# A two-layer hybrid encoder on one core: Gelu's polynomial on ScalarE, one softmax pass for both key heads, and other warm-up products

## The chip, the cores and the metric

The kernel runs on one core of a Trainium2 chip. The metric is the device time of one execution in microseconds (us), as the median of several runs. A core has TensorE (PE in the rows; its weight loads are PEld), VectorE (DVE), ScalarE (ACT), GpSimd (POOL) and SyncE (SP), which issues the transfers. Each engine works off its own list of instructions in order, and waits on semaphores where an input, or a buffer to write into, isn't ready.

## The reference

Two layers over 512 prompt frames and 8 x 16 sample frames, width 1024, all in float32. Each layer normalizes, projects, sends three parts of the projection through three mixers, projects back, and adds a squared-ReLU MLP:

```
def _hybrid_layer(x, ...):
    proj = _rms_norm(x, norm1) @ w_in                       # 1024 -> 1536
    out_a = _rglru_mixer(u_a, g_a, ...)                     # h * gelu(gate)
    out_b = _s5_mixer(u_b, ...)                             # z = gelu(y); z * sigmoid(z @ w_glu + b)
    out_c = _swa_prompt / _swa_cached(_rope(q), _rope(k), v, sinks)
    x = x + concat([out_a, out_b, out_c]) @ w_out
    x = x + square(relu(_rms_norm(x, norm2) @ w_up)) @ w_down

def _sink_softmax(scores, sinks, mask):
    m = max(max(scores), s);  e = exp(scores - m)
    return e / (sum(e) + exp(s - m))
```

Attention has 8 query heads and 2 key heads (4 query heads on each), chunks of 64 frames, and a window of the chunk itself and the two before it. `gelu` is the tanh form: 0.5 x (1 + tanh(0.798 (x + 0.0447 x^3))).

## The kernel before

**Tiling.** The frames are cut into two groups g of 320 columns (256 of the prompt, 64 of the samples). Activations lie with features on the 128 partitions. A product of one weight tile of 1024 x 128 with a group (`product`, L246) is 24 matmuls of 128x128 by 320 columns: weights and activations are each split into a rounded part and a rest (wh and wl; ScalarE copies wh at L243, VectorE subtracts for wl at L244), and three of the four cross products are added over 8 tiles of the inner dimension. There are 336 such products, 8064 of these matmuls ("mm" in the rows), the same in both kernels.

**Stages.** Layer 0: `in_proj` of group 0 (12 products), its mixers, `in_proj` of group 1 (12 more; 576 matmuls in all), its mixers, `out_proj` of group 0 (8 products), a first quarter of group 0's MLP, `out_proj` of group 1, and the rest of the MLP. Layer 1 does the same, with its first projection and group 0's mixers laid over the end of layer 0's MLP. The mixers are `lru` (L641), `s5` (L694) and `attention` (L788). An output-projection product reads the mixers' result `mix` in eight tiles: tiles 0 to 3 hold the two recurrent mixers, 4 to 7 attention's heads. A product can so begin its first 12 matmuls before attention is done, and three products can do this at once, since the PSUM tag "mm" has three banks.

**Attention** works in chunks cq = 0 to 3 of a group, and on two pairs of samples (hf). `probs(cq, kv)` makes the scores of one key head (L878), and `soft` (L814) the softmax over them: maxima (L818), the negated maximum with the sink (L820 or L822), two exponentials with their sums (L824), the sink's exponential (L826, or L828 and L829), the sum and its reciprocal (L830, L831), and two multiplications, one on VectorE and one on GpSimd (L833). `turned(cq, kv)` transposes the probabilities on TensorE (L176) and copies them back (L890 or L892); `values(cq)` multiplies them by the values (L899) and writes `mix` (L903, L904). The PSUM tag "att", with two banks, serves scores, transposes, values and the gates of `lru` (L663).

**Gelu** (`gelu2`, L542) is called 16 times, on 128x320: two gates and two S5 outputs for each group of each layer. It takes three VectorE operations (L545 to L547), a ScalarE tanh (L548) and a last VectorE operation (L549).

**Setup.** Layer 0's constants for S5 are made on VectorE, GpSimd and TensorE in the first 130 us, beside the projections. Twelve products of a zeroed 128x128 tile (L990) run on TensorE before the first weights arrive.

**Order.** The program is built by a scheduler that plans each engine's list from the code's order and from its own estimates of times. A change in one place so reorders the lists around it.

## Time and profile before

| | |
|---|---|
| median of 3 runs | 1457.65 us (1455.84 to 1466.05) |
| span of the profiled execution | 1454.2 us |
| TensorE busy | 1404.7 us (97%) |
| TensorE weight loads | 1336.3 us (92%) |
| VectorE busy | 924.5 us (64%) |
| ScalarE busy | 662.4 us (46%) |
| GpSimd busy | 377.0 us (26%) |
| mean granted TensorE clock | 0.979 |

The span reaches from the first to the last instruction; a run's time holds a few us more. "Busy" counts the time in which at least one instruction of the engine is under way. TensorE's matmuls overlap, so a busy share of 97% doesn't mean that it does 97% of what it could; how many matmuls a stretch holds tells that. The granted clock is 1.00 at 2.4 GHz and 0.50 at 1.2 GHz.

### The profile page before, as it was taken

The numbers are of one execution on the slowest core, as the hardware profiler recorded it, in microseconds if no ns is written. First come the engines' busy times: TensorE is split into PE (matmuls) and PEld (weight loads), VectorE is DVE, ScalarE is ACT, GpSimd is POOL, SyncE is SP. The second block draws the span as 40 slices with busy tenths as digits, with TensorE's granted clock in tenths as the row PEclk, the third lists the DMA queues.
The fourth block names the chain that finished last, engine by engine and source line by source line (L and its number), as shares of the span: only waits on it lengthen the run. The fifth ranks groups of instructions, "written<-read, shape, count | busy, mean of one in ns | idle before, by whom it ended". The sixth has DMA issues, their size and how long they took to land.

```text
span 1454.2 us, 25829 instructions
## 1 busy us (share of the span) xinstructions
PE 1404.7 (97%) x9540; PEld 1336.3 (92%) x9540; DVE 924.5 (64%) x1858; ACT 662.4 (46%) x1387; POOL 377.0 (26%) x565
## 2 busy tenths in 40 slices
PE   7699999999999999999999999999999999999997
PEld 7688688899999999999987898789999999999997
DVE  8999889856544344357687768875664434434564
ACT  6566565545422122135674667453543312313543
POOL 3847269401010011072244225320110100100111
PEclk9999899999999999999998999899999999999998
DMA  6232122344422222234422342224443222223452
GB/s 244 86 109 81 50 95 97 105 150 140 152 80 78 76 80 73 73 107 157 140 91 73 120 137 92 68 95 145 149 146 106 73 73 73 80 78 104 153 174 94
DMA packets 91389, 156.27 MB, mean 107 GB/s; under 512 B 14336, under 2 KB 18304, under 8 KB 91264
## 3 DMA queue, kind: packets, MB, share of 16 engines
q1 hardware_dynamic: 91264, 154.63, 32.0%
q8 instruction: 75, 1.23, 0.4%
q14 instruction: 50, 0.41, 0.1%
HBM read 151.02 MB, written 3.37 MB: 106 GB/s over the span
## 4 chain that ended last, share of the span: by engine, by line
PE 80%; DVE 11%; POOL 4%; issue 3%; ACT 2%; DMA 1%; SPq 0%; DVEq 0%; POOLq 0%
PE mm L254 24%; PE mm L252 24%; PE mm L253 24%; DVE wl L244 2%; PE att L899 1%; PE att L878 1%; PE s L755 1%; PE s L753 1%; PE att L176 1%; PE s L176 1%; PE fin L326 0%; PE att L663 0%; PE s L721 0%; PE s L779 0%; DVE bigr L269 0%
## 5 line engine op out<-in xcount | busy, mean ns | idle before, releaser
L254 PE MATMUL mm<-bigr,wl 128*128 128x320 f32 x2688 | 840.9, 314 | 22.6 <-DVE wl L244 22.6
L252 PE MATMUL mm<-bigr,wh 128*128 128x320 f32 x2688 | 840.2, 313 | 1.7 <-ACT wh L243 1.1
L253 PE MATMUL mm<-bigr,wh 128*128 128x320 f32 x2688 | 839.1, 313 | 1.0 <-DVE bigr L269 1.0
L243 ACT ACTIVATE wh<-raw 128x512 fp32r<-128x512 f32 x544 | 340.7, 630 | 494.4 <-PE mm L253 469.9
L254 PEld LDWEIGHTS mm<-bigr,wl 128*128 128x128 f32 x2688 | 509.8, 190 | 34.7 <-DVE wl L244 27.4
L252 PEld LDWEIGHTS mm<-bigr,wh 128*128 128x128 f32 x2688 | 509.4, 190 | 7.9 <-issue 5.0
L253 PEld LDWEIGHTS mm<-bigr,wh 128*128 128x128 f32 x2688 | 509.5, 190 | 6.9 <-issue 3.9
L244 DVE TENSOR_TENSOR wl<-raw,wh 128x512 fp32r<-128x512 f32 x544 | 399.7, 736 | 179.6 <-ACT wh L243 158.9
L156 POOL TENSOR_SCALAR bigr<-t 128x320 fp32r<-128x320 f32 x128 | 63.0, 493 | 566.3 <-ACT t L952 566.3
L934 DVE TENSOR_TENSOR xT<-xT,mm 128x320 f32<-128x320 f32 x160 | 77.7, 486 | 127.5 <-PE mm L254 127.4
L952 ACT ACTIVATE t<-t 128x320 f32<-128x320 f32 x128 | 59.9, 470 | 137.9 <-DVE t L951 132.3
L954 DVE TENSOR_TENSOR bigr<-t,bigr 128x320 fp32r<-128x320 f32 x128 | 69.7, 546 | 69.6 <-POOL bigr L156 69.3
L951 DVE SCALAR_TENSOR_TENSOR t<-mm,r 128x320 f32<-128x320 f32 x124 | 60.6, 488 | 81.5 <-PE mm L254 81.4
L288 POOL TENSOR_TENSOR ss<-ss,sq 128x320 f32<-128x320 f32 x58 | 56.9, 981 | 195.7 <-ACT sq L281 185.6
L833 POOL TENSOR_SCALAR att<-att,st 128x192 f32<-128x192 f32 (+3 forms) x40 | 37.2, 931 | 79.5 <-DVE st L831 43.6
L824 ACT ACTIVATE att<-att,st 128x192 f32<-128x192 f32 (+3 forms) x80 | 30.7, 389 | 28.3 <-DVE st L822 22.1
L269 DVE SCALAR_TENSOR_TENSOR bigr<-xT,sm,bigr 128x320 fp32r<-128x320 f32 x64 | 39.7, 629 | 3.8 <-ACT bigr L268 3.6
L268 ACT ACTIVATE bigr<-xT,sm 128x320 fp32r<-128x320 f32 x64 | 34.4, 558 | 11.1 <-DVE xT L934 7.8
L281 ACT ACTIVATE sq<-xT 128x320 f32<-128x320 f32 x66 | 30.4, 460 | 9.9 <-DVE xT L934 3.7
L878 PE MATMUL att<-kT,q 64*64 64x192 f32 (+2 forms) x256 | 28.1, 329 | 2.5 <-ACT att L824 2.1
L605 POOL TENSOR_TENSOR sw<-sw,cs 128x320 f32<-128x320 f32 x20 | 19.4, 969 | 33.6 <-ACT sw L604 28.3
L176 PE MATMUL att<-ident,att 128*128 128x128 f32 (+1 forms) x144 | 24.6, 280 | 3.2 <-DVE att L833 1.0
(287 smaller groups left out, 1078.6 us busy)
## 6 DMA issues: line engine op xcount, KB each, us to landing
raw<-w_up SPq DMA_DIRECT2D x192, 256.0 KB, 2.6
raw<-w_down SPq DMA_DIRECT2D x192, 256.0 KB, 2.6
raw<-w_in SPq DMA_DIRECT2D x96, 256.0 KB, 2.6
raw<-w_out SPq DMA_DIRECT2D x64, 256.0 KB, 2.5
xT<-x SPq DMA_DIRECT2D x8, 320.0 KB, 5.7
yT<-xT SPq DMA_DIRECT2D x8, 320.0 KB, 2.5
cs<-rope SPq DMA_DIRECT2D x4, 320.0 KB, 4.4
gg<-gg SPq DMA_DIRECT2D x2, 512.0 KB, 5.1
```

What stands on the lines that cost most here:

```text
L156: return G.tensor_scalar(out, in_, 1.0, 0.0, OP.mult, OP.add)
L176: PE.transpose(out, in_, ident[0:n, 0:n])
L243: act(h, raw, AF.Copy)
L244: tt(l, raw, h.bitcast(F32), OP.subtract)
L252: mm(pt, lhsT=h[:, k % 4], rhs=m[:, k, 0], start=k == 0, stop=False)
L253: mm(pt, lhsT=h[:, k % 4], rhs=m[:, k, 1], start=False, stop=False)
L254: mm(pt, lhsT=l[:, k % 4], rhs=m[:, k, 0], start=False, stop=k == 7)
L288: G.tensor_tensor(self.ss, self.ss, sq, OP.add)
L934: tt(xT[:, g, k], xT[:, g, k], pt, OP.add)
L951: V.scalar_tensor_tensor(t, pt, 0.0, norm.r, OP.max, OP.mult)
L952: act(t, t, AF.Square)
L954: tt(am[:, f, 1], t, am[:, f, 0].bitcast(F32), OP.subtract)
```

## The change

Three edits. `gelu2` takes a ScalarE square with a scale, one VectorE operation, the tanh and the last VectorE operation, so two VectorE operations fewer and one ScalarE operation more in each call. `soft` takes the scores of both key heads (or of both pairs of samples) in a list: it keeps a maximum for each, and does the small operations on four columns at once in place of two. `sprobs` and `probs` therefore make both sets of scores, in both "att" banks, before the softmax, and the calls at the end of `attention` are reordered. The warm-up is now 20 products over a zeroed tile of 640 columns, which GpSimd clears and ScalarE copies first.

```
@@ gelu2
-        eng.tensor_tensor(w, x, x, OP.mult)
-        eng.tensor_scalar(w, w, 0.044715, 1.0, OP.mult, OP.add)
-        eng.tensor_tensor(w, w, x, OP.mult)
+        act(w, x, AF.Square, scale=math.sqrt(0.044715))
+        eng.scalar_tensor_tensor(w, w, 1.0, x, OP.add, OP.mult)
         act(w, w, AF.Tanh, scale=0.7978845608028654)
         V.scalar_tensor_tensor(out, w, 1.0, x, OP.add, OP.mult)
@@ soft(b, x, sk, nsk, one): b and x are now lists
-            st4 = tp.tile([128, 5, 2], F32, tag="st4", name="st4", bufs=4)
+            st4 = tp.tile([128, 5, 4], F32, tag="st4", name="st4", bufs=2)
-            V.reduce_max(mx, b, axis=AX.X)
+            n2 = 2 * len(b)
+            for m in range(len(b)):
+                V.reduce_max(mx[:, 2 * m:2 * m + 2], b[m], axis=AX.X)
...
-            for n in range(2):
-                act(x[:, n], b[:, n], AF.Exp, scale=0.125, bias=nm[:, n:n + 1], accum_out=den[:, n:n + 1])
+            for n in range(n2):
+                act(x[n // 2][:, n % 2], b[n // 2][:, n % 2], AF.Exp, scale=0.125, bias=nm[:, n:n + 1], accum_out=den[:, n:n + 1])
...
-            for n in range(2):
-                (G if n else V).tensor_scalar(x[:, n], x[:, n], rd[:, n:n + 1], None, OP.mult)
+            for n in range(n2):
+                v = x[n // 2][:, n % 2]
+                (G if n % 2 else V).tensor_scalar(v, v, rd[:, n:n + 1], None, OP.mult)
@@ probs(cq): both key heads, scores in both banks; sprobs() likewise for both pairs of samples
+            bs = [bank3("att", 2, 256) for kv in range(2)]
...
+            soft([b[:, :, 0:nk] for b in bs], [pe[:, :, st:256] for pe in pes], skp[:, L], nskp[:, L], False)
@@ end of attention
-        sprobs(0)
-        sprobs(1)
-        sturned(0)
-        probs(0, 0)
-        sturned(1)
-        svalues(0)
-        svalues(1)
-        probs(0, 1)
+        sprobs()
+        for hf in range(2):
+            sturned(hf)
+        for hf in range(2):
+            svalues(hf)
+        probs(0)
         for cq in range(4):
             for kv in range(2):
                 turned(cq, kv)
-                if cq < 3:
-                    probs(cq + 1, kv)
+            if cq < 3:
+                probs(cq + 1)
             values(cq)
@@ warm-up
-    for _ in range(12):
+    zr = bigr()
+    zr = zr[:, 0:1].rearrange("p a b c -> p (a b c)")
+    G.memset(tab[:, 512:1152], 0.0)
+    act(zr, tab[:, 512:1152], AF.Copy)
+    for n in (512, 384, 320, 256, 128):
+        for _ in range(4):
+            mm(warm[:, 0:n], lhsT=zr[:, 0:128], rhs=zr[:, 0:n], start=True, stop=True)
+    for _ in range(0):
         mm(warm[:, 0:128], lhsT=Mm[...], rhs=Mm[...], start=True, stop=True)
```

Two places show how the lists move. The first is TensorE's list in layer 0 while group 0's attention ends. All 576 input-projection matmuls and the first half of one output-projection product stand ahead of it. `att<-ident,att` are transposes of probabilities, `att<-kT,q` scores, `att<-att,vt` values; rows beginning with `s` in the second name are S5's. Before:

```order
L176 MATMUL att<-ident,att 128x128 x4
L176 MATMUL s_1206<-ident,bigf 128x80 x4
L779 MATMUL s_1226<-bigf,gg 128x320
L878 MATMUL att<-kT,q 64x192 x4
L899 MATMUL att<-att,vt 64x256 x4
L779 MATMUL s_1230<-bigf,gg 128x320
L176 MATMUL att<-ident,att 128x128 x4
L779 MATMUL s_1226<-bigf,gg 128x320
L779 MATMUL s_1230<-bigf,gg 128x320
```

The changed kernel, from the scores of the third chunk (cq = 2) to the first of those of the fourth:

```order
L884 MATMUL att<-kT,q 64x192 x8
L176 MATMUL s_1214<-ident,bigf 128x80 x4
L778 MATMUL s_1233<-bigf,gg 128x320
L778 MATMUL s_1237<-bigf,gg 128x320
L905 MATMUL att<-att,vt 64x256 x2
L778 MATMUL s_1233<-bigf,gg 128x320
L778 MATMUL s_1237<-bigf,gg 128x320
L176 MATMUL att<-ident,att 128x128 x5
L176 MATMUL s_2096<-ident,ub 80x128 x4
L176 MATMUL att<-ident,att 128x128 x3
L176 MATMUL s_2102<-ident,ub 80x128 x4
L884 MATMUL att<-kT,q 64x192 x4
```

Before, this piece holds the last scores of the fourth chunk, and that chunk's alone come behind the 576 matmuls; now those of both heads of the third chunk and of the fourth do. Between the third chunk's scores and the transposes that need its softmax stand four S5 transposes, four S5 products and two value products.

The second place is VectorE's list at the S5 outputs of the same group, where Gelu and softmax stand side by side. Before:

```order
L545 TENSOR_TENSOR gw<-bigf 128x320
L546 TENSOR_SCALAR gw<-gw 128x320
L547 TENSOR_TENSOR gw<-gw,bigf 128x320
L818 TENSOR_REDUCE st_1452<-att 128x2
L549 SCALAR_TENSOR_TENSOR bigf<-gw,bigf 128x320
L822 SCALAR_TENSOR_TENSOR st_1452<-st_1452,nskp 128x2
L828 TENSOR_TENSOR st_1452<-sm,st_1452 128x2
L892 COPY att<-att 128x512
L762 SCALAR_TENSOR_TENSOR bigf<-ub,sm,s_1206 128x320
L830 TENSOR_TENSOR st_1452<-st_1452 128x2
```

After:

```order
L819 TENSOR_REDUCE st_1404<-att 128x2 x2
L761 SCALAR_TENSOR_TENSOR bigf<-ub,sm,s_1214 128x320
L823 SCALAR_TENSOR_TENSOR st_1404<-st_1404,nskp 128x4
L829 TENSOR_TENSOR st_1404<-sm,st_1404 128x4
L546 SCALAR_TENSOR_TENSOR gw<-gw,bigf 128x320
L831 TENSOR_TENSOR st_1404<-st_1404 128x4
L832 RECIPROCAL st_1404<-st_1404 128x4
L548 SCALAR_TENSOR_TENSOR bigf<-gw,bigf 128x320
L835 TENSOR_SCALAR att<-att,st_1404 128x192 x2
```

One Gelu stands there with two VectorE rows in place of four, and one softmax with four columns serves both key heads, with two reductions ahead of it and two multiplications behind.

## Rows read from the trace of the kernel before

**Rows 1.** Page, part 2: busy tenths and granted clock in 40 slices of 36.4 us.

```profile
DVE  8999889856544344357687768875664434434564
PEclk9999899999999999999998999899999999999998
```

**Rows 2.** Windows: stretch, us, each engine's busy us (instructions), granted clock, DMA.

```profile
77.00:147.00 70.00, 65.90 (x469) 59.02 (x468) 68.64 (x167) 47.87 (x120) 43.05 (x62) 0.93 0.29 92
151.00:161.00 10.00, 9.67 (x51) 7.38 (x52) 8.10 (x23) 4.88 (x17) 3.00 (x7) 0.50 0.32 105
161.00:181.00 20.00, 19.67 (x132) 13.45 (x131) 15.28 (x40) 10.04 (x27) 2.66 (x4) 1.00 0.04 14
200.00:252.00 52.00, 48.02 (x324) 41.50 (x323) 51.59 (x85) 26.87 (x69) 47.19 (x58) 0.90 0.28 89
472.61:509.00 36.39, 36.39 (x250) 36.39 (x249) 11.81 (x21) 6.33 (x10) 0.00 (x0) 1.00 0.24 76
```

**Rows 3.** TensorE's waits, 0 to 150 us: who waited for whom, total, times, longest.

```profile
PE mm L254 <- DVE wl L244: 14.2, 12, 2.7
```

**Rows 4.** TensorE's waits from 740 to 990 us (layer 1's mixers).

```profile
PE mm L254 <- DVE wl L244: 3.0, 1, 3.0
```

**Rows 5.** Lines, VectorE, 0 to 300 us: count, busy us, mean ns, idle before.

```profile
L818 DVE TENSOR_REDUCE st<-att 128x2 f32<-128x384 f32 x12 | 6.6, 549 | 2.2 <-PE att L878 2.2
L830 DVE TENSOR_TENSOR st<-st 128x2 f32<-128x2 f32 x20 | 5.9, 297 | 0.9 <-ACT st L829 0.9
L822 DVE SCALAR_TENSOR_TENSOR st<-st,nskp 128x2 f32<-128x2 f32 x16 | 4.7, 292 | 0.1
L828 DVE TENSOR_TENSOR st<-sm,st 128x2 f32<-128x2 f32 x16 | 3.8, 239 | 0.2
L546 DVE TENSOR_SCALAR gw<-gw 128x320 f32<-128x320 f32 x8 | 3.3, 410 | 0.1
L831 DVE RECIPROCAL st<-st 128x2 f32<-128x2 f32 x20 | 3.2, 158 | 0.3
L545 DVE TENSOR_TENSOR gw<-t 128x320 f32<-128x320 f32 x4 | 2.4, 596 | 0.1
```

**Rows 6.** Lines, ScalarE, 60 to 300 us.

```profile
L824 ACT ACTIVATE att<-att,st 128x192 f32<-128x192 f32 x24 | 9.8, 413 | 12.0 <-DVE st L822 10.1 <-DVE rsq L309 1.8
L824 ACT ACTIVATION_READ_ACCUMULATOR att<-att,st 128x1 f32 x40 | 7.8, 196 | 0.0
L281 ACT ACTIVATE sq<-xT 128x320 f32<-128x320 f32 x7 | 3.2, 463 | 2.5 <-DVE xT L934 2.1 <-POOL tab L436 0.4
```

**Rows 7.** Timeline: two heads' softmaxes, first and last rows; TensorE behind the second (start, duration).

```profile
103.69 0.28 DVE L818 TENSOR_REDUCE st<-att 128x2 f32<-128x128 f32 x1
112.70 0.84 POOL L833 TENSOR_SCALAR att<-att,st 128x64 f32<-128x64 f32 x1 [0.26 <-DVE st L831]
...
165.62 0.56 DVE L818 TENSOR_REDUCE st<-att 128x2 f32<-128x384 f32 x1 [1.45 <-PE att L878]
170.26 0.76 POOL L833 TENSOR_SCALAR att<-att,st 128x192 f32<-128x192 f32 x1 [8.45 <-PE att L878]
172.67 1.34 PE L779 MATMUL s<-bigf,gg 128*128 128x320 f32 x4
```

**Rows 8.** Timeline, two neighbouring products at the lower clock.

```profile
158.58 0.47 PE L254 MATMUL mm<-bigr,wl 128*128 128x320 f32 x1
158.84 0.47 PE L252 MATMUL mm<-bigr,wh 128*128 128x320 f32 x1
```

**Rows 9.** Timeline of the start: the warm-up, and TensorE's waits behind it.

```profile
1.75 0.53 POOL L216 MEMSET Mm<- 128x512 f32 x1
2.33 5.39 PE L990 MATMUL fin<-Mm 128*128 128x128 f32 x24 [2.33 <-POOL uap L647]
...
18.27 0.42 PE L254 MATMUL mm<-bigr,wl 128*128 128x320 f32 x1 [1.56 <-DVE wl L244]
```

More of the change, by code (lines that the diff above doesn't have):

```diff
@@ L831, in soft, with sprobs @@
             V.reciprocal(rd, rd)
-            for n in range(2):
-                (G if n else V).tensor_scalar(x[:, n], x[:, n], rd[:, n:n + 1], None, OP.mult)
-        def sprobs(hf):
-            b = bank3("att", 2, 256)
-            for i in range(2):
-                for kv in range(2):
-                    mm(b[64 * kv:64 * kv + 64, i, 0:144], lhsT=q.qS[64 * kv:64 * kv + 64, 2 * hf + i].rearrange("p i t -> p (i t)"),
-                       rhs=kcT[64 * kv:64 * kv + 64, hf, i], start=True, stop=True)
-            soft(b[:, :, 0:144], p[hf], sks[:, L:L + 1], nsks[:, L:L + 1], True)
+            for n in range(n2):
+                v = x[n // 2][:, n % 2]
+                (G if n % 2 else V).tensor_scalar(v, v, rd[:, n:n + 1], None, OP.mult)
+        def sprobs():
+            bs = [bank3("att", 2, 256) for hf in range(2)]
+            for hf, b in enumerate(bs):
+                for i in range(2):
+                    for kv in range(2):
+                        mm(b[64 * kv:64 * kv + 64, i, 0:144], lhsT=q.qS[64 * kv:64 * kv + 64, 2 * hf + i].rearrange("p i t -> p (i t)"),
+                           rhs=kcT[64 * kv:64 * kv + 64, hf, i], start=True, stop=True)
+            soft([b[:, :, 0:144] for b in bs], p, sks[:, L:L + 1], nsks[:, L:L + 1], True)
         def sturned(hf):
@@ L867, in geo, with probs @@
             return j, ((1,) if j == 0 else (0, 1)), nk, 64 * max(cc - 2, 0), 256 - nk, 64 - 64 * ch
-        def probs(cq, kv):
+        def probs(cq):
             j, kts, nk, k0, st, w0 = geo(cq)
-            pe, ps, q0 = pes[kv], slice(64 * kv, 64 * kv + 64), 64 * cq
+            q0 = 64 * cq
             if cq == 0:
-                G.memset(pe[:, :, 0:64], 0.0)
-                G.memset(pe[:, :, 256:320], 0.0)
-            b = bank3("att", 2, 256)
+                for pe in pes:
+                    G.memset(pe[:, :, 0:64], 0.0)
+                    G.memset(pe[:, :, 256:320], 0.0)
+            bs = [bank3("att", 2, 256) for kv in range(2)]
             for pr in range(2):
                 for s in range(2):
-                    mm(b[64 * s:64 * s + 64, pr, 0:nk], lhsT=q.q[ps, 2 * pr + s, q0:q0 + 64], rhs=kT[ps, k0:k0 + nk], start=True, stop=True)
-            soft(b[:, :, 0:nk], pe[:, :, st:256], skp[:, L, 2 * kv:2 * kv + 2], nskp[:, L, 2 * kv:2 * kv + 2], False)
+                    for kv, b in enumerate(bs):
+                        ps = slice(64 * kv, 64 * kv + 64)
+                        mm(b[64 * s:64 * s + 64, pr, 0:nk], lhsT=q.q[ps, 2 * pr + s, q0:q0 + 64], rhs=kT[ps, k0:k0 + nk], start=True, stop=True)
+            soft([b[:, :, 0:nk] for b in bs], [pe[:, :, st:256] for pe in pes], skp[:, L], nskp[:, L], False)
         def turned(cq, kv):
```

## The prediction

> **What bounds the kernel now.** I read the page's slices first, then windows by stage, then TensorE's waits, and last the groups of instructions and a timeline. The slices [rows 1] show VectorE at nine tenths or near it for the first 290 us and at 5 to 8 tenths from 650 to 1020 us (both times the mixers run), and mostly at 3 to 5 elsewhere. In the MLP stretches TensorE does nothing but its products: 250 in 36.39 us, one each 145.6 ns [rows 2]. For 8064 of them that is 1174 us that no part of this change touches. What the change can move lies where the mixers run.
>
> There the windows [rows 2] show two kinds of stretch. From 77 to 147 us VectorE is busy 68.6 of 70 us and from 200 to 252 us 51.6 of 52: here a VectorE operation less is time, as far as TensorE's waits for VectorE's weight parts bear it out (14.2 us in 12 waits before 150 us [rows 3]). From 161 to 181 us VectorE has 4.7 us free, and TensorE runs small S5 and attention products almost without a gap (19.7 of 20 us). So the first layer decides, and in it two stretches bound by VectorE with one between them that is bound by the chain of attention and S5.
>
> **Gelu.** A call loses L545 and L546, 0.60 and 0.41 us as they measure in the first 300 us [rows 5]; L547 is replaced by an operation on the same two inputs, which I price the same. That is 1.0 us of VectorE a call, 8.1 us for layer 0's eight calls. ScalarE gets a square of 128x320, 0.46 us [rows 6]; it is busy 47.9 of 70 us in the tightest stretch [rows 2], so this lies in its idle time. The square takes the place of two VectorE operations in the chain to the tanh, so the chain is no longer.
>
> The same square on VectorE took 0.60 us against 0.46 on ScalarE. The Trainium skill ("ScalarE: Activation LUTs", Rules for kernel authors) says the opposite of this edit: multiply on VectorE and not on ScalarE, VectorE being up to about three times faster in bf16. Were ScalarE three times slower here, eight calls would cost it about 8 us more in layer 0; in this float32 kernel the rows show no such factor, and the sum goes by the rows.
>
> **Softmax.** Forty calls become twenty on four columns. Each pair loses one of L822, L828, L830 and L831: 0.29 + 0.24 + 0.30 + 0.16 = 1.0 us in layer 0 [rows 5], ten pairs, 9.9 us at the most; four columns I price as two, since these operations are far too short for columns to matter. Maxima, exponentials and multiplications stay.
>
> **What of it pays before the last input projection.** What matters is VectorE's list ahead of the last weight part of `in_proj` for group 1 (the 48th L244). Before, two Gelus and six softmaxes stand ahead of it; after, two Gelus and two shared softmaxes, which are four of the six. Removed: 2 x 1.0 for Gelu, 1.7 for the two shared passes. The other two softmaxes, chunk 1's, now stand behind it: two reductions of at most 0.55 us, two times the 1.0 us of small operations, two multiplications and a value subtraction, each about as long as L546: 4.3 us, a little less since this chunk's scores are narrower; I count 4. Together 7.7 us by durations, which for short operations overlap in part. The stretch before 147 us is bound by VectorE almost throughout, so I take 6.8 us, with 4 and 8 as ends (4 if TensorE's own small products become the limit there).
>
> **What the moved chunk costs.** The deferred work lands in the stretch that the attention chain ends. In TensorE's list two whole chunks now follow the 576 input-projection matmuls, each as scores, one softmax for both heads, eight transposes. One head's softmax there takes 5.4 us from the maxima to the end of GpSimd's multiplication (165.62 to 171.02 [rows 7]). Both together need one more reduction (0.55), two more exponentials with their accumulator reads (2 x 0.61) and one more GpSimd multiplication (0.76) [rows 5 to 7], about 2.5 us; 7.5 us with a little less queueing. Between the third chunk's scores and its transposes TensorE's list holds four S5 transposes, four S5 products and two value products: ten small matmuls, the S5 products at 0.27 us (four end in 1.34 [rows 7] with the last one's tail), the others at half of that: 1.9 us. TensorE so stands for 5.6 us, where before the two heads' chains covered each other and it stood hardly at all. If nothing queues, the durations alone of one head's steps add up to 3.3 us (0.55 + 0.29 + 2 x 0.61 + 0.30 + 0.16 + 0.76), and the wait to 3.9; if VectorE is as full as at 103.69 to 113.54, 9.9 us for a head [rows 7], to 10.5. At the fourth chunk the list holds two dozen weight products (3.5 us) and S5 work, and the wait is 1 to 2 us. I take 7.2 us for both, 4 to 12 as ends. Behind TensorE waits everything that needs `mix`, so all of `out_proj` for group 0.
>
> **The second stretch bound by VectorE**, 200 to 252 us: two of the Gelu calls and one or two softmax passes stand in it, 2 to 3 us, and I take 2.5. TensorE loses 4 us there to waits and spacing (48.0 of 52), so work that arrives late from the stall above finds a part of its time again; I credit 1.5 us, between 0 and 4.
>
> **Layer 1.** TensorE waits little there: the longest is 3.0 us, on a weight part [rows 4]. Less VectorE work may shorten that. Against it, the first transposes of the samples now need both pairs' softmax, some 2 us more than one pair's, in each of two groups. Nothing net, with 4 us either way.
>
> **Clock.** In 151 to 161 us the clock is at its lower level, 0.50 [rows 2], and products are 0.26 us apart [rows 8] in place of 0.1456 [rows 2]. Ten such microseconds cost 4.4 where TensorE is dense. A new stand of 5 us may bring one such fall, a shorter in-projection may remove this one. I put +1, from -4.4 to +4.4. [...]
>
> **Warm-up.** It starts later: GpSimd clears 640 columns behind Mm (0.53 x 640/512 = 0.66, to 2.9 us), ScalarE copies them (under 2 x 0.46 us [rows 6], to 3.8 us). Its 6400 columns at the lower clock's 0.26 us for 320 [rows 8] are 5.2 us, to 9 us where the warm-up ended at 7.7. TensorE then waits 1.56 us for VectorE at 18.27 anyway [rows 9], and that takes up the 1.3 us. I price it at 0, with +3 if the clock stays low for the first two dozen products (24 x 0.11).
>
> **Sum.** -6.8 + 7.2 - 2.5 - 1.5 + 0 + 1 = -2.6 on a span of 1454.2, so 1451.6. The median of the runs lies 3.4 us over that span; I predict 1455 us.
>
> **Rivals.**
> *The savings are paid in full.* The chain in the middle stays hidden, because VectorE, less loaded, answers at once (3.3 us for a head) and other work is there. Then -6.8 + 2 - 2.5 - 2 in layer 1 - 2 of clock: -11, 1446; with every term at its end, -18, 1440. For it speaks that VectorE has 4.7 of 20 us free there; against it, that the list leaves 1.9 us of work between scores and transposes. Chance 0.25.
> *Attention becomes the bound (slower).* Both banks are taken by one softmax, so scores, transposes and values of the two heads no longer overlap. With 11 us in the middle stretch, one clock fall more (+4), and 2 us more at four later chunks, of group 1 and of layer 1, where the list has left too little between (+8), against -6.8: +16, 1474. It decides from about 9 us for the shared softmax. For it speaks the 9.9 us that one head took where VectorE was full [rows 7], though that lies ahead of 147 us; against it, that in layer 1 MLP products are there to fill. Chance 0.17.
> *It does nothing that counts, and the warm-up costs.* TensorE's own small products, not VectorE, limit 77 to 147 us; the gain is 3 and the chain 5, the clock rises one step late (+3): 1462. Chance 0.10.
>
> **Chances and range.** The forecast case, 1449 to 1461, 0.48. About 1% (14.6 us) is what a measurement of this kernel can tell from no change. Faster than 1443 takes most of the first rival's ends: 0.13. Slower than 1472 takes the upper half of the second and a tail: 0.13. Within, 0.74. The range, 1443 to 1469, leaves 0.10 below and above.
>
> **What would show it.** Right: VectorE's busy time falls by some 30 us (16 x 1.0 + 20 x 1.0 at the most); the 48th L244 comes about 7 us earlier than 146 us; TensorE has one wait of 4 to 7 us on L832 or L835 some 15 us later, with the lower clock behind it; `out_proj` starts at much the same time as before. Wrong: no such wait (first rival), several of them in both layers (second), or the 48th weight part no earlier (third).

## The result and the profile after

The changed kernel takes 1439.99 us (median of 4 runs, 1439.3 to 1443.42) where the kernel before, on the same chip, takes 1457.06: a ratio of 0.9886, with a 95% interval of 0.986 to 0.9911. The profiled execution spans 1437.8 us (before 1454.2), so 16.4 us are gone. The prediction, 1455 us with a range down to 1443, lies above it: the time came out 3 us under the range, on the side of the first rival (the savings are paid in full), though not where that rival put them.

| | before | after |
|---|---|---|
| span of the profiled execution | 1454.2 us | 1437.8 us |
| TensorE busy | 1404.7 us | 1391.3 us |
| VectorE busy | 924.5 us | 905.4 us |
| ScalarE busy | 662.4 us | 665.1 us |
| mean granted TensorE clock | 0.979 | 0.984 |

The page's slices of the changed kernel, VectorE's busy tenths and the granted clock, answer [rows 1]:

```profile
DVE  8999789756544344357678768865664434434564
PEclk9999899999999999999999999999999999999998
```

VectorE is not much emptier than before. The windows that answer [rows 2] (stretch, length, busy us and instructions of TensorE, its weight loads, VectorE, ScalarE and GpSimd, granted clock, transfers):

```profile
77.00:147.00 70.00, 63.13 (x457) 56.41 (x456) 69.26 (x149) 45.14 (x106) 45.30 (x61) 0.95 0.29 89
161.00:181.00 20.00, 19.34 (x130) 13.60 (x129) 14.29 (x35) 14.26 (x43) 4.98 (x6) 0.85 0.08 27
200.00:252.00 52.00, 47.70 (x322) 41.32 (x321) 46.17 (x75) 29.14 (x71) 51.28 (x68) 0.93 0.29 90
```

TensorE's waits, 0 to 150 us (the first two rows, answering [rows 3] and, for the warm-up, [rows 9]) and 740 to 990 us (answering [rows 4]): who waited for whom, us, times, longest:

```profile
PE mm L254 <- DVE wl L244: 14.8, 12, 4.0
PE fin L999 <- ACT bigr L996: 3.7, 1, 3.7
...
PE mm L254 <- DVE wl L244: 1.8, 1, 1.8
PE att L860 <- DVE att L852: 1.2, 1, 1.2
PE att L176 <- DVE att L835: 1.1, 2, 0.6
```

The groups of VectorE's lines from 0 to 300 us that answer [rows 5]: the Gelu operation that is left, and the softmax's small operations on four columns.

```profile
L823 DVE SCALAR_TENSOR_TENSOR st<-st,nskp 128x4 f32<-128x4 f32 x8 | 2.5, 306 | 0.1
L546 DVE SCALAR_TENSOR_TENSOR gw<-gw,bigf 128x320 f32<-128x320 f32 x4 | 2.1, 516 | 1.8 <-ACT gw L545 1.8
L829 DVE TENSOR_TENSOR st<-sm,st 128x4 f32<-128x4 f32 x8 | 1.9, 232 | 0.1
```

Four columns cost what two did (0.31 against 0.29 us on L823, 0.23 against 0.24 on L829).

**Where the time went.** Both programs run the same 8064 weight matmuls (L252 to L254) in the same order, so the start of the n-th of them in the two traces tells when the time was won, at places where as much of the other work is done in both. The 3900th, where layer 1's mixers begin to stand between the products, is such a place (748 small matmul records lie ahead of it in each kernel): it starts 4.1 us earlier (726.3 to 722.2). The 5184th, where they end, is 16.0 earlier, and so is the last. So layer 0 gave 4 us and layer 1 12. Inside layer 0 the shift says little, since the lists put the small matmuls in other places: the 574th starts 0.6 us later (149.5 to 150.2), the 577th, the first behind all input projections, 8.2 earlier (158.8 to 150.6) with 28 fewer small records ahead of it, the 601st 6.2 earlier, the 613th 0.6 later. Below, "layer 0" is the shift of the 3900th, and "layer 1" the time from the 3900th to the 5184th: 289.1 us before, 277.1 after. In layer 1's stretch TensorE also runs small matmuls (scores, transposes, values, S5), which the traces show as 656 records in each kernel; "small" below is the time on them, from each start to TensorE's next start, so that a wait, and a stretch at the lower clock, count with the matmul that they fall on.

All runs in one table. The runs were made on several chips, so medians of different rows compare by their ratios, which are to the kernel before, timed beside each, with 95% intervals. The columns on layers come from one profile of each kernel. How far such a number moves by itself shows in kernels whose layer 1 has the same edits: `before`, `warm_only` and `warm16` lie at 287.9 to 289.1 us, and the change, `no_warm`, `kv_outer` and `share_pad` at 276.7 to 277.8. Under 2 us a difference in layer 1 says nothing.

| kernel | median us | ratio | layer 0, shift | layer 1 | small |
|---|---|---|---|---|---|
| before | 1457.06 | | 0 | 289.1 | 77.9 |
| after | 1439.99 | 0.9886 (0.986 to 0.9911) | -4.1 | 277.1 | 69.8 |
| gelu_only | 1451.2 | 0.9968 (0.9952 to 0.9985) | +2.4 | 284.2 | 77.9 |
| soft_only | 1441.23 | 0.9902 (0.9885 to 0.9919) | -8.1 | 282.0 | 71.9 |
| warm_only | 1468.17 | 1.0087 (1.0064 to 1.011) | +9.9 | 289.1 | 78.0 |
| no_warm | 1439.64 | 0.9882 (0.9857 to 0.9908) | -6.6 | 276.7 | 69.9 |
| kv_outer | 1439.21 | 0.9885 (0.9867 to 0.9904) | -4.2 | 277.8 | 71.3 |
| warm16 | 1468.45 | 1.0069 (1.0041 to 1.0097) | +7.7 | 287.9 | 79.0 |
| gelu_dve | 1452.85 | 0.997 (0.9949 to 0.9992) | -3.5 | 288.9 | 78.6 |
| apart | 1451.27 | 0.9954 (0.9938 to 0.9969) | -2.7 | 286.6 | 80.9 |
| share_pad | 1442.73 | 0.9897 (0.9874 to 0.9921) | -0.7 | 277.4 | 69.7 |
| mix | 1438.65 | 0.9871 (0.9848 to 0.9895) | -7.4 | 278.3 | 70.7 |
| mix_kv | 1440.54 | 0.9884 (0.9856 to 0.9911) | -2.2 | 277.9 | 71.3 |
| pair_all | 1441.81 | 0.9891 (0.986 to 0.9922) | -4.7 | 277.5 | 68.1 |
| split | 1452.06 | 0.9968 (0.9949 to 0.9987) | +5.6 | 280.9 | 74.3 |
| pair_s5 | 1453.99 | 0.9975 (0.996 to 0.999) | +3.1 | 284.6 | 73.9 |
| pair_mix | 1437.57 | 0.9864 (0.9848 to 0.9879) | -0.6 | 273.2 | 66.8 |
| apart_pair | 1439.84 | 0.9889 (0.9852 to 0.9926) | -1.3 | 276.5 | 70.4 |

### The profile page after: what moved, and what is told of

Read it like the earlier page. It is cut to its first block, busy times and chain, and to the rows that moved or that the text cites. A ratio compares the mean times of both kernels' runs of the same rounds, so it can differ in the third digit from the quotient of the medians.

```text
span 1437.8 us, 25702 instructions
## 1 busy us (share of the span) xinstructions
PE 1391.3 (97%) x9536; PEld 1324.8 (92%) x9536; DVE 905.4 (63%) x1750; ACT 665.1 (46%) x1384; POOL 378.0 (26%) x566
## 4 chain that ended last, share of the span: by engine, by line
PE 81%; DVE 10%; POOL 4%; issue 2%; ACT 2%; DMA 1%; DVEq 0%; SPq 0%; ACTq 0%; POOLq 0%
PE mm L254 24%; PE mm L252 24%; PE mm L253 24%; DVE wl L244 2%; PE att L884 1%; PE att L905 1%; PE att L176 1%; DVE bigf L738 1%; PE s L754 1%; PE s L752 1%; DVE bigr L269 1%; PE att L860 1%; POOL att L835 1%; PE fin L326 1%; PE s L176 0%
## 5 line engine op out<-in xcount | busy, mean ns | idle before, releaser
L254 PE MATMUL mm<-bigr,wl 128*128 128x320 f32 x2688 | 838.5, 313 | 19.4 <-DVE wl L244 19.2
L252 PE MATMUL mm<-bigr,wh 128*128 128x320 f32 x2688 | 838.5, 313 | 0.7 <-ACT wh L243 0.5
L254 PEld LDWEIGHTS mm<-bigr,wl 128*128 128x128 f32 x2688 | 507.9, 189 | 30.2 <-DVE wl L244 24.2
L252 PEld LDWEIGHTS mm<-bigr,wh 128*128 128x128 f32 x2688 | 507.8, 189 | 7.6 <-issue 5.0
L244 DVE TENSOR_TENSOR wl<-raw,wh 128x512 fp32r<-128x512 f32 x544 | 399.2, 736 | 176.4 <-ACT wh L243 157.9
L938 DVE TENSOR_TENSOR xT<-xT,mm 128x320 f32<-128x320 f32 x160 | 77.9, 487 | 127.7 <-PE mm L254 127.5
L955 DVE SCALAR_TENSOR_TENSOR t<-mm,r 128x320 f32<-128x320 f32 x124 | 60.6, 489 | 80.9 <-PE mm L254 80.7
L288 POOL TENSOR_TENSOR ss<-ss,sq 128x320 f32<-128x320 f32 x58 | 58.6, 1010 | 176.8 <-ACT sq L281 170.6
L281 ACT ACTIVATE sq<-xT 128x320 f32<-128x320 f32 x66 | 30.4, 461 | 9.0 <-POOL ss L288 4.8
L176 PEld LDWEIGHTS att<-ident,att 128*128 128x128 f32 (+1 forms) x144 | 16.9, 136 | 8.1 <-POOL att L835 2.7
```

Source lines behind the costliest of these rows:

```text
L176: PE.transpose(out, in_, ident[0:n, 0:n])
L244: tt(l, raw, h.bitcast(F32), OP.subtract)
L252: mm(pt, lhsT=h[:, k % 4], rhs=m[:, k, 0], start=k == 0, stop=False)
L254: mm(pt, lhsT=l[:, k % 4], rhs=m[:, k, 0], start=False, stop=k == 7)
L288: G.tensor_tensor(self.ss, self.ss, sq, OP.add)
L938: tt(xT[:, g, k], xT[:, g, k], pt, OP.add)
```

## The experiments

**The three edits one by one.** Each is applied alone to the kernel before; `no_warm` is the change without its warm-up.

```
gelu_only:  only the hunk of gelu2          soft_only:  only soft, sprobs, probs and the calls
warm_only:  only the hunk of the warm-up    no_warm:    the change, warm-up hunk taken back
```

> The kernel before with the Gelu edit alone. Theory A, score products and waits: the changed kernel gained 16 us on the span, of which the score products (L878, now L884) show 6.9 us less on TensorE and layer 1's waits and lower clock most of the rest; Gelu is then a small part, and this kernel is 0 to 4 us under the kernel before. Theory B, VectorE's shorter list: Gelu takes 16 calls x 0.8 to 1.0 us, about as much as the softmax edit, off VectorE, so this kernel is 7 to 9 us faster. Theory C, the scheduler's new order: any edit moves the lists, so it may come out anywhere from 5 us faster to 5 us slower.

> The kernel before with the softmax edit alone (shared small operations, scores of both heads in turn, the new order of calls). Theory A: 11 to 15 us faster, nearly all of the change. Theory B: 7 to 10 us faster, the other half being Gelu's. Theory C: not the sum of anything; the two edits alone don't add up to 17.

> The kernel before with the new warm-up alone. Theories A and B: within 2 us of the kernel before, since the first product starts 0.7 us later and TensorE has caught up at its 25th product, as the trace of the change shows. Theory C: the lists behind it move, and up to 5 us either way may come of it.

> The changed kernel with the old warm-up: Gelu and softmax edits together. If the edits add up, 4.7 + 14.3 = 19 us under the kernel before, 1437, and the new warm-up costs 3 us in the change. In layer 1 the two edits added up so far (4.9 and 7.0 us against 12.0), so 12 us there by every theory. Theory D: the warm-up itself costs 12 us, so 1428. Theory C: layer 0 comes out anywhere from 8 us faster to 8 us slower than before, so 1437 to 1453.

On the whole time, `gelu_only` (4.9 us under the kernel before beside it) fell between theories A and B, `soft_only` (14.8 under) in A's range, `no_warm` (19.0 under) on the sum of the two, and `warm_only` (12.1 over) outside every theory's range.

In layer 1 the edits add up: Gelu alone -4.9 us, softmax alone -7.1, both -12.4 (`no_warm`) and -12.0 (the change). In layer 0 they don't: Gelu alone +2.4, softmax -8.1, the warm-up +9.9, the sum of the three +4.2, and the change -4.1. The warm-up alone costs 0.9%, and all of that in layer 0. The windows from 151 to 180 us, of the kernel before:

```profile
151.00:180.00 29.00, 28.34 (x178) 20.44 (x178) 22.59 (x62) 14.18 (x42) 5.41 (x10) 0.83 0.14 46
```

and of `warm_only`:

```profile
151.00:180.00 29.00, 25.91 (x126) 17.47 (x125) 15.95 (x44) 9.80 (x33) 5.80 (x10) 0.59 0.10 28
```

TensorE gets through 126 matmuls where it did 178, at a mean clock of 0.59 for 0.83. Nothing of the warm-up runs there; what differs is the order in which the scheduler laid out the work.

**Is it the warm-up, or any new order?** `warm16` is the kernel before with four of its own products more.

```
-    for _ in range(12):
+    for _ in range(16):
```

> The kernel before with 16 of its own warm-up products in place of 12, and nothing else. The new warm-up alone made the kernel 12 us slower, all of it in layer 0 around and behind group 0's attention, where the lower clock and waits for weight parts grew. Theory C, the scheduler's order: four products more shift its plan's start and give another list for every engine in layer 0, so this kernel also moves by 4 us or more, in the same stretch, though its warm-up is the old one. Theory D, the new warm-up itself (the copy on ScalarE, the extra tile, the products): this kernel stays within 2 us of the kernel before.

Four products of about 0.45 us each (twelve take 5.39 us [rows 9]) make the first weight matmul 1.2 us later, which is made good by the 25th; yet layer 0 ends 7.7 us later, and layer 1 takes nothing more. VectorE's operations start in another order from the 30th on. So four products more, which cost nothing by the 25th matmul, move layer 0 by their new order alone, and what `warm_only` loses need not be the price of the new products. (Which place in the new order costs the time was not looked for.)

**The order of the score products** was changed along with the softmax edit; `kv_outer` puts one key head's ahead of the other's again.

```
-    for pr in range(2):
-        for s in range(2):
-            for kv, b in enumerate(bs):
+    for kv, b in enumerate(bs):
+        for pr in range(2):
+            for s in range(2):
```

> The changed kernel with one loop turned: probs makes the four score products of one key head and then those of the other, where the change takes the two heads in turn. Both softmaxes are still shared. Theory A: neighbouring products that use different halves of the partitions overlap on TensorE and those of one head don't, so the time per chunk goes back from about 0.6 to 0.8 us or more, and the kernel gives back 4 to 7 us: 1444 to 1447. Theory B: VectorE's list is the same, so the time is that of the change, 1440, within 1 us. Theory C: up to 5 us either way.

1439.21 against 1439.99 us, ratios of 0.9885 and 0.9886: no difference. Theory A had 4 to 7 us more. The last section shows why it got none: the two heads' scores overlap in this order too.

**Gelu without ScalarE's square.** `gelu_dve` is the kernel before with two VectorE operations for the polynomial, both on VectorE.

```
-        eng.tensor_tensor(w, x, x, OP.mult)
-        eng.tensor_scalar(w, w, 0.044715, 1.0, OP.mult, OP.add)
-        eng.tensor_tensor(w, w, x, OP.mult)
+        eng.scalar_tensor_tensor(w, x, 0.044715, x, OP.mult, OP.mult)
+        eng.scalar_tensor_tensor(w, w, 1.0, x, OP.add, OP.mult)
```

> The kernel before with Gelu's polynomial in two VectorE operations and none on ScalarE: one VectorE operation fewer in each call, where the change has two fewer and one ScalarE operation more. If VectorE's time in layer 1 is what the Gelu edit gained there (4.9 us), about half of it, 2 to 3 us, comes here; if the gain is that the polynomial's first step left VectorE's list altogether and so waits behind nothing there, nothing. Layer 0 may move by some us either way by its order.

One VectorE operation fewer in each call gives 0.2 us in layer 1; two fewer, with the square on ScalarE, give 4.9. Windows of layer 1's first 60 us, before:

```profile
720.00:780.00 60.00, 56.71 (x409) 50.44 (x408) 51.27 (x99) 41.26 (x96) 30.18 (x37) 0.94 0.30 98
```

and with `gelu_only`:

```profile
720.00:780.00 60.00, 57.98 (x430) 52.82 (x428) 48.88 (x93) 42.60 (x96) 28.73 (x33) 0.97 0.30 99
```

TensorE does 21 matmuls more there, about 3 us, at a clock of 0.97 for 0.94. In the table the small matmuls are unchanged (77.9), so Gelu's gain is in the spacing of the weight products. Part of it is the clock: over all of layer 1 the mean granted clock is 0.965 before and with `gelu_dve`, and 0.976 with `gelu_only`, which is some 20 and 14 us at 1.2 GHz. Products are 0.26 us apart there in place of 0.146 [rows 8, rows 2], so 7 us fewer are worth some 3 of the 4.9 us, by this estimate. Why the two edits differ in the clock, and what the rest is, I can't settle from these runs.

**Is it the sharing?** `apart` is the change with the softmax's small operations per head, the scores of both heads still issued in one call.

```
-            soft([b[:, :, 0:nk] for b in bs], [pe[:, :, st:256] for pe in pes], skp[:, L], nskp[:, L], False)
+            for kv, b in enumerate(bs):
+                h2 = slice(2 * kv, 2 * kv + 2)
+                soft([b[:, :, 0:nk]], [pes[kv][:, :, st:256]], skp[:, L, h2], nskp[:, L, h2], False)
```

> The changed kernel with the small operations of the softmax done for each head (and each pair of samples) by itself, as before, while the scores of both heads still come first and the calls stand in the new order. 76 short VectorE operations and 20 ScalarE exponentials are back. Theory B, the number of VectorE operations: layer 1 gives back most of the 7 us that the softmax edit gained there, and layer 0 several us. Theory E, the grouping: taking both heads' scores, transposes and values together keeps TensorE's small products close behind each other, and that alone gains; then layer 1 stays within 2 us of the change.

Layer 1 gives back 9.5 of its 12 us. I first read that as what the small operations cost. The next runs show that reading to be wrong.

**VectorE's time put back.** `share_pad` adds four VectorE operations behind each shared softmax, whose result nothing uses.

```
             V.reciprocal(rd, rd)
+            for _ in range(4):
+                tt(dum[:, 0], den[:, 0:2], rd[:, 0:2], OP.mult)
```

> The change, with four VectorE multiplications of 128x2 behind the reciprocal in each of the 20 shared softmaxes (their result is used by nothing). VectorE so has the operation count of the softmax per head again, while a softmax still goes once through VectorE's queue. Theory B1 (VectorE's time is what sharing saves): 10 of these softmaxes stand in layer 1, 40 operations of 0.16 to 0.30 us are 6 to 12 us of VectorE, and layer 1 gives back most of the 9.5 us that separate the kernel 'apart' from the change, so layer 1 takes 284 us or more where the change takes 277. Theory B2 (the shorter way through the queue saves it: one wait for the exponentials in place of two): layer 1 stays within 2 us of the change's 277. The whole time is read together with layer 0, whose part moves by some us with any new order: B1 1446 to 1452, B2 1437 to 1445.

Layer 1 takes 277.4 us against the change's 277.1, with 40 of these operations in it. The group in `share_pad`, from 800 to 1010 us:

```profile
L835 DVE TENSOR_TENSOR dum<-st 128x2 f32<-128x2 f32 x28 | 7.8, 280 | 0.3
```

The 40 of layer 1 take 10.8 us of VectorE. So VectorE's time is not what layer 1 was paid for (B1 falls).

**What differs on TensorE.** In the table the small matmuls take 78 to 81 us in every kernel with the softmax per head and 70 to 72 in every one with it shared, as long as no operation was added to make or break pairs (`split` and the `pair` kernels below). The number is the same, 656, and so is the work. Timelines of TensorE in layer 1 show it: S5's first products and the scores, with the product behind the first, before:

```profile
886.33 1.11 PE L721 MATMUL s<-bigf,Bm 64*128 64x80 f32 x8
887.38 0.46 PE L839 MATMUL att<-att,qS 64*64 64x144 f32 x2
...
922.97 0.87 PE L878 MATMUL att<-kT,q 64*64 64x192 f32 x8
```

and after:

```profile
882.32 1.41 PE L720 MATMUL s<-bigf,Bm 64*128 64x80 f32 x16
883.65 0.42 PE L254 MATMUL mm<-bigr,wl 128*128 128x320 f32 x1
...
909.01 0.88 PE L884 MATMUL att<-kT,q 64*64 64x192 f32 x16
```

Eight S5 records take 1.05 us to the next instruction, sixteen in one run 1.33; eight score records show 0.87 us, sixteen 0.88. (Each of these matmuls is two records, so eight records are four matmuls.) These products use 64 of the 128 rows: one half of a set, or one key head, the upper rows, the other the lower. Where both stand next to each other in TensorE's list, it works them at the same time. Two sets apart so cost some 0.75 us more than two sets together, and a shared softmax brings them together, since it needs both heads' scores before anything else can go on. That is theory F. The Trainium skill ("TensorEngine Tiling (Array Packing)", Key Properties) has this: different tiles of the array can load weights and multiply in parallel; these rows agree.

**Pairs taken away, and pairs made.** `split` is the change with a one-element copy that makes the second head's scores, and S5's second half, wait for the first; its loops are turned for this, one head's (or half's) products first, which by itself did nothing for the scores (`kv_outer`). `pair_all` is the change with two one-element operations so that neither set can begin before both banks are free. `pair_s5` is the kernel before with these for S5 alone.

```
split:
+                if kv:                                                  # and likewise: if r, for S5
+                    V.tensor_copy(bs[1][0:1, 0, 0:1], bs[0][0:1, 1, 0:1])
pair_all, behind bs = [...] of probs and of S5 (pair_s5: of S5):
+            V.memset(bs[1][0:1, 0, 0:1], 0.0)
+            V.tensor_copy(bs[0][0:1, 0, 0:1], bs[1][0:1, 0, 0:1])
```

> The change, with a VectorE copy of one element from the first bank to the second between the two key heads' scores and between S5's two halves (L720), so that the second set waits for the first: in TensorE's list every run of these products has 4, none 8. The softmax stays shared. Theory F: three S5 and three score pairs of layer 1 are lost at 0.75 us each, the small matmuls take 74 to 76 us where the change takes 69.8, and layer 1 rises by 4 to 7 us. Theory B2: the small matmuls stay at 70 or nearly, and layer 1 rises by 2 us at the most, for 16 more small VectorE operations. Whole time by F 1444 to 1452, by B2 1438 to 1444.

> The change, with two VectorE operations on one element ahead of each chunk's scores and of each half of S5's first products (a memset in the second bank, a copy of it to the first), so that neither set can begin before both banks are free. In TensorE's list all the score products of layer 1 then stand in runs of 8 or as 5 and 3 (in the change: three runs of 8 and ten of 4) and the S5 products (L720) in four runs of 8 (two of 8 and two of 4 beside one of 8). Theory F (TensorE works two sets of products of 64 rows at the same time when they stand next to each other on opposite halves of the rows; the trace shows 16 S5 matmuls in 1.34 us in one run where 8 take 1.05, and 16 score matmuls in 0.81 where 8 take 0.80): five or so more pairs at 0.75 us each, layer 1's 656 small matmuls take 65 to 67 us where the change takes 69.8, and layer 1 falls by 2 to 4 us. Theory B2 (the softmax's shorter way through VectorE's queue is what the softmax edit gains, and grouping is nothing): the small matmuls stay at 70, and layer 1 stays or rises by a few us for the scores that wait for two banks. Whole time by F 1434 to 1442, by B2 1438 to 1448, layer 0's order with it.

> The kernel before, with the two one-element operations ahead of S5's halves alone: the S5 products (L721 there) stand in four runs of 8 in layer 1, where before has one of 8 and six of 4. Softmax, Gelu and warm-up as before. Theory F: three pairs at 0.75 us, layer 1's small matmuls 75 to 76 us where before takes 77.9, and layer 1 falls by 2 to 3 us. Theory B2: nothing in layer 1, within 1 us. Whole time 1450 to 1462, since layer 0's order changes with it.

The groups of TensorE's lines in layer 1's stretch (count of records, busy us in all, mean ns of one, idle before), before:

```profile
L878 PE MATMUL att<-kT,q 64*64 64x192 f32 x96 | 10.9, 336 | 0.0
L721 PE MATMUL s<-bigf,Bm 64*128 64x80 f32 x64 | 8.1, 280 | 0.0
```

after:

```profile
L884 PE MATMUL att<-kT,q 64*64 64x192 f32 x96 | 9.6, 335 | 0.0
L720 PE MATMUL s<-bigf,Bm 64*128 64x80 f32 x64 | 6.4, 280 | 0.0
```

`split`:

```profile
L888 PE MATMUL att<-kT,q 64*64 64x192 f32 x96 | 11.1, 352 | 0.0
L722 PE MATMUL s<-bigf,Bm 64*128 64x80 f32 x64 | 8.9, 280 | 0.0
```

`pair_s5`:

```profile
L880 PE MATMUL att<-kT,q 64*64 64x192 f32 x96 | 13.6, 365 | 0.1
L723 PE MATMUL s<-bigf,Bm 64*128 64x80 f32 x64 | 4.5, 279 | 1.5 <-DVE st L833 1.0 <-DVE s L720 0.5
```

`pair_all`:

```profile
L888 PE MATMUL att<-kT,q 64*64 64x192 f32 x96 | 6.0, 369 | 0.0
L722 PE MATMUL s<-bigf,Bm 64*128 64x80 f32 x64 | 4.5, 279 | 0.8 <-ACT wh L243 0.8
```

One record takes the same in all of them (0.28 us for S5), and the 64 of them together between 4.5 and 8.9 us, by how many run at once. `split` raises layer 1 by 3.8 us, just under what F expected and above B2's 2. `pair_s5` lowers S5's from 8.1 to 4.5 and layer 1 by 4.5, more than F's 2 to 3; but its scores take 2.7 us more in their new order (13.6 for 10.9), so its 4.5 us are not S5's pairs alone. In `pair_all` both groups together fall by 5.5 us against the change, and yet layer 1 doesn't fall (277.5) by the 2 to 4 us that F expected: TensorE's waits there grow from 4.1 to 7.9 us in all. The largest two, from 724 to 1004 us (who waited for whom, us, times, longest):

```profile
PE s L756 <- DVE bigf L745: 3.3, 2, 2.0
PE att L176 <- DVE att L837: 2.0, 2, 1.2
```

The change waits 1.8 us at the most in one place (above). The mean granted clock is lower too, 0.975 in layer 1 for the change's 0.982. So pairs that make TensorE wait can cost what they bring.

**Pairs without the sharing.** `apart_pair` is `apart` with `pair_all`'s operations: a softmax for each head, and nearly all pairs made.

> The kernel 'apart' (the change with the softmax's small operations per head), with the two one-element operations of 'pair_all' ahead of each chunk's scores and of S5's halves, so that in layer 1 seven of the eight chunks' score products stand in a run of 8, the last as two of 4, and S5's in four runs of 8. Theory F alone (all that sharing gains in layer 1 is the pairing that comes with it): the score and S5 products fall from 21.7 us to about 12, and layer 1 comes to within 3 us of the change: 277 to 280 where 'apart' takes 286.6. Theory F with another half (pairing is worth 4 to 5 of the 9.5 us, as in 'split', and the two passes through VectorE's queue the rest): layer 1 at 280 to 284. Pairs are not the cause: 285 or more. Whole time 1442 to 1452, with layer 0's order.

The groups in `apart`:

```profile
L885 PE MATMUL att<-kT,q 64*64 64x192 f32 x96 | 11.6, 353 | 0.0
L720 PE MATMUL s<-bigf,Bm 64*128 64x80 f32 x64 | 8.1, 280 | 0.0
```

and in `apart_pair`:

```profile
L889 PE MATMUL att<-kT,q 64*64 64x192 f32 x96 | 5.5, 337 | 0.0
L722 PE MATMUL s<-bigf,Bm 64*128 64x80 f32 x64 | 4.5, 279 | 1.4 <-DVE s L719 1.4
```

The two groups fall by 9.7 us, and layer 1 by 10.1, from 286.6 to 276.5 us, to where the change is, a little below theory F's 277 to 280; the whole kernel falls to 1439.84, under the range of 1442 to 1452, with every small operation of the softmax done per head. Neither waits nor clock can be the reason: TensorE's waits in layer 1 are 6.8 us in both kernels, and the granted clock is lower in the faster one (0.963 for 0.976). So pairs alone can bring as much as the shared softmax does in layer 1. It is not shown that the change itself gets its 9.5 us over `apart` by pairs alone. It has fewer of them than `apart_pair`, and they account for 3.8 by `split`. What the rest is, is open.

**Clock and waits.** Before and after differ in these too. Windows of layer 1, before (that of 720 to 780 us stands above):

```profile
900.00:1000.00 100.00, 97.01 (x660) 84.76 (x660) 74.61 (x156) 51.94 (x128) 29.11 (x38) 0.95 0.28 92
```

and after:

```profile
720.00:780.00 60.00, 58.10 (x437) 52.33 (x436) 50.10 (x90) 40.84 (x97) 27.97 (x38) 0.97 0.31 98
900.00:1000.00 100.00, 100.00 (x694) 90.33 (x695) 68.88 (x140) 50.77 (x121) 19.90 (x27) 0.98 0.33 109
```

Over all of layer 1 the mean granted clock is 0.965 before and 0.982 after, some 20 and 10 us at 1.2 GHz. Ten such microseconds fewer are worth 4.4 us where TensorE is dense (products 0.26 us apart for 0.146), so up to that much of the 12.0 us may be the clock; this is an estimate, and part of it lies in the column "small". Before, the clock fell at 912.0 us in the wait of 3.0 us and at 772.1 behind one of 1.7 us, and once more 10 to 20 us after each; after, only twice, behind waits of 1.8 and 1.2 us. But the parts don't simply add up: `no_warm` has only some 3 us at 1.2 GHz (mean clock 0.994), its waits are 6.0 us for the change's 4.1, and its layer 1 is the same within 0.4 us.

**A better version?** `mix` takes the softmax edit in both layers, the Gelu edit in layer 1 alone, and the old warm-up; `mix_kv` is `mix` with `kv_outer`'s order; `pair_mix` is `mix` with `pair_all`'s operations.

```
+        if L == 0:
             eng.tensor_tensor(w, x, x, OP.mult)
...
+        else:
+            act(w, x, AF.Square, scale=math.sqrt(0.044715))
...
```

> Softmax for both heads in both layers, the warm-up of before, and Gelu's square on ScalarE in layer 1 alone. If the effects of the two edits add up in layer 1 and layer 0's part depends on the order alone, layer 0 is that of the softmax alone (8.1 us less than before by the end of its mixers) and layer 1 has both (12 us less): a span 19 to 21 us below before, 1434 to 1436, and a median of 1437 to 1439, a little below the change. If layer 0's gain with the softmax alone was an accident of its order that this edit upsets, the median lies at 1440 to 1448.

> As mix, with the score products of one key head ahead of those of the other, as before the change. The order of the score products did nothing measurable in the change itself (1439.2 against 1440.0 us), so the same is expected here: within 4 us of mix, the difference being layer 0's order and its low-clock stretches, layer 1 within 2 us of mix.

> The kernel 'mix' (softmax for both heads, Gelu's square on ScalarE in layer 1 alone, the warm-up of before) with the pairing of pair_all. By theory F it gains in layer 1 over mix what pair_all gains over the change, 2 to 4 us, and is the fastest of all, 1433 to 1438. By B2 it is at 1437 to 1445.

`mix` and `mix_kv` came out as expected, and `pair_mix` in F's range. All three land within 3 us of the change. `pair_mix` has the lowest median, 1437.57, and the shortest layer 1, 273.2; its layer 0 gives most of that back (+6.8 against `mix`). Its interval (0.9848 to 0.9879) overlaps the change's, so it beats the kernel before but is not shown to beat the change.

## Why the prediction was wrong, step by step

- **Before the last input projection, -6.8: this step failed too.** The sign that I had named for it, the 48th L244 about 7 us earlier, came out as 1.0 us:

```profile
146.30 2.05 DVE L244 TENSOR_TENSOR wl<-raw,wh 128x512 fp32r<-128x512 f32 x1
145.29 0.66 DVE L244 TENSOR_TENSOR wl<-raw,wh 128x512 fp32r<-128x512 f32 x1
```

  It ends 2.4 us earlier, and the matmul that waits for it, the 567th, starts 2.4 us earlier (148.41 to 146.01). What stood ahead of it in VectorE's list I had read rightly: two Gelus and six softmaxes before, two and two shared ones after, and their durations, with one value subtraction, fell from 15.8 to 6.9 us. But the other 326 operations ahead of it, the same in both kernels, took 157.5 us in all where they took 150.3, so by durations 1.7 us are left of the 8.9. Why they took longer is open. Fewer VectorE operations saved little of its time here.
- **The moved chunk, +7.2: the form was wrong, and its size can't be read.** What the moved chunk cost the traces don't tell, since the lists around it differ as well (28 small records fewer ahead of the 577th matmul). No wait of 4 to 7 us appears, as the first rival had it. The shared softmax runs from 162.67 to 168.68, 6.0 us where I took 7.5, and TensorE fills it, since its small matmuls go at half speed:

```profile
161.08 1.57 PE L884 MATMUL att<-kT,q 64*64 64x192 f32 x16
162.67 1.02 DVE L819 TENSOR_REDUCE st<-att 128x2 f32<-128x384 f32 x2 [4.15 <-PE att L884]
163.17 2.47 PE L778 MATMUL s<-bigf,gg 128*128 128x320 f32 x4
167.02 1.66 POOL L835 TENSOR_SCALAR att<-att,st 128x192 f32<-128x192 f32 x2 [10.05 <-DVE st L832]
167.35 1.34 PE L778 MATMUL s<-bigf,gg 128*128 128x320 f32 x4 [0.66 <-DVE bigf L548]
```

  Four S5 records take 2.47 us here and 1.34 four microseconds later, and the 16 score records 1.57 where the rows of layer 1 above show 0.88. I had priced ten small matmuls at 1.9 us, at the full clock, and had misread a row for it: the four records that end in 1.34 us are two S5 products and not four, so that the ten would take some 3 us at the full clock. The one wait shown is of 0.66 us. Part of the lost time is there as a low clock.
- **200 to 252 us, -2.5 and -1.5, clock +1.** By the end of layer 0 the shift is -4.1, where the terms of the sum gave -2.6. That this fits is luck: its first term failed, its second took another form, and with other orders of nearly the same work layer 0 lies between -8.1 and +9.9 (table). My sum had no term for that, and the range, from -12 to +14 about the forecast, had to carry it.
- **Layer 1, "nothing net, with 4 us either way": this step failed.** It was -12.0, nearly all of what the sum missed. I looked for a wait that less VectorE work could shorten, found one of 3.0 us [rows 4], and stopped. That wait did shrink, to 1.8 us, and all waits of that stretch together by 2.2 (6.3 to 4.1). What I had not asked is how many of TensorE's small matmuls run at once: 3.8 us by `split`. That hangs on what stands side by side in its list, not on the amount of work, and the busy share of TensorE near 97% hides it, since one matmul or two at the same time both count as busy. Nor had I priced the lower clock behind the waits, which layer 1 has too: 4.4 us by the estimate above. These overlap and don't make up the whole, so the split of the 12.0 us is in part open. The rival that was right in its total (1440 with every term at its end) had 2 us for layer 1 too.
- **Gelu's and softmax's durations: right; VectorE's busy time: not.** By the groups of the whole run the small softmax operations fall from 36.1 to 15.0 us and Gelu's from 31.7 to 17.2, 35.6 together, as priced. The busy time falls by 19.1 and not by 30, since the other 1642 operations took 9.3 us longer in all, and the rest is overlap. `share_pad` shows that in layer 1 the difference buys nothing.
- **The square on ScalarE: the price for VectorE was a mean with an outlier in it.** L545 takes 0.47 us on ScalarE, as the estimate from L281 said [rows 6]. On VectorE it took not 0.60 [rows 5] but 0.48 to 0.49 in 14 of the 16 calls; the other two took 0.93 and 0.95, and one of them is among the four calls of that row:

```profile
L545 DVE TENSOR_TENSOR gw<-t x8: 475/483/925, 77.8 to 882.6; 128x320 f32<-128x320 f32 x8
```

  (least, median and greatest ns). So the square costs the same on either engine, and moving it takes its whole time off VectorE. The rule of the Trainium skill that the prediction weighed ("ScalarE: Activation LUTs", Rules for kernel authors: multiply on VectorE) gives its factor for bf16; this float32 square shows none.
- **Warm-up, 0: right by itself.** TensorE starts on it 3.7 us into the span, as its wait above says, the first weight matmul comes at 8.2 us where it came at 7.5, and the 25th at 12.65 against 12.72. But any edit here also draws a new order, and that was worth +9.9 and +7.7 us in two cases. "Nothing" was a price for the products, not for the edit.
- **The slower rival** needed the shared softmax to stand for 9 us; it took 6.0.
- **The chances** don't agree with each other: faster than 1443 us got 0.13 in one sentence and 0.10 in the next. The measured time lies there, 3 us outside the range.

## What to carry to other kernels

A TensorE that is nearly always busy can still be won time from: count what stands together in its list, and bring products that use opposite halves of the rows next to each other, if need be by two one-element operations that make both wait for the same thing, and look whether TensorE then waits more. When a scheduler orders the work, apply an edit that should do nothing (here four warm-up products) to learn how far the order alone moves the time, and read edits by stage, where they add up, before the total. To tell whether an engine's time is what was paid for, put it back as operations that nothing uses. Read single durations beside a mean before it becomes a price, and count how many records one instruction leaves.

## What the runs showed of the hardware that I had not expected

- Two sets of matmuls on opposite halves of the rows can cost nearly as much as one: 16 score records in 0.88 us and 8 in 0.87, 16 S5 records in 1.33 us and 8 in 1.05. In `kv_outer` the scores gain this too, though all four products of one head stand ahead of the other's in the list:

```profile
910.08 0.89 PE L884 MATMUL att<-kT,q 64*64 64x192 f32 x16
```

- The granted clock can be at its lower level while TensorE is dense: in the changed kernel from 151 to 161 us TensorE is busy 9.52 of 10 us, and the mean clock is 0.79.

```profile
151.00:161.00 10.00, 9.52 (x55) 6.74 (x53) 6.03 (x15) 5.03 (x19) 3.82 (x8) 0.79 0.26 86
```

  The clock fell at 156.9 us. In the six microseconds before, TensorE ran weight products, values, S5's small matmuls and transposes, and no wait in the ten before was over 0.3 us. Whether the small matmuls are the reason wasn't tried.
